# A one-core mixer-and-FFN layer: modulation rows turned by a transpose before they are stored, first convolution taps moved from VectorE to ScalarE, two blocks of modulation sums moved to TensorE, and one gate's sums moved later

## The chip, the core and the metric

The kernel runs on one core of a Trainium2 chip. The metric is the device time of one execution in microseconds (us). Before the change the median of three runs is 2446.79 us (2441.33 to 2446.85). The names of the engines in the profile are PE (TensorE matmul), PEld (TensorE's weight load, which runs beside matmuls), DVE (VectorE), ACT (ScalarE), POOL (GpSimd) and SP (SyncE, whose queue issues nearly all DMAs here).

## What is computed

One layer acts on x of 2048 tokens by 1024 features, steered by one vector c of 1024. Silu of c times a 1024 x 6144 matrix gives six modulation rows; a second matrix gives two more for the closing norm.

```
c_act = silu(c)
shift_m, scale_m, gate_m, shift_f, scale_f, gate_f = split(c_act @ w_ada + b_ada, 6)
h = rms_norm(x, g_mix) * (1 + scale_m) + shift_m
gate_b, gate_c, h_conv, q, k, v, z, a, bt = split(h @ w_in)
ya = grouped_rms(gate_b * conv3(gate_c * h_conv))
q, k, v = split(silu(conv4([q, k, v])))           # causal, depthwise
o = chunked_gated_delta_rule(l2(q), l2(k), v, g(a), sigmoid(bt))
yb = rms_norm(o) * silu(z)
x = x + gate_m * ([ya, yb] @ w_out)
h = rms_norm(x, g_ffn) * (1 + scale_f) + shift_f
x = x + gate_f * ((silu(h @ w_gate) * (h @ w_up)) @ w_down)
out = rms_norm(x, g_final) * (1 + scale_o) + shift_o
```

All tensors are float32. A product is made of three passes over a high and a low part of each operand (high by high, high by low, low by high), so each weight tile is first cast on ScalarE (`whi`, L367) and its rest taken on VectorE (`wlo`, L369).

## The kernel before

**Stages.** The mixer works on four blocks of 512 tokens (`for b in range(NB)`, about 0 to 1114 us of the profile), then come the gate-and-up products of the feed-forward part (to about 1982 us) and the down products. In a block the projections come strip by strip, a strip being the 128 output features of one 1024 x 128 piece of `w_in`: four of k, four of q, four of v, four of z, then twelve for the gated convolution, then the output product. A strip is 24 matmuls of 128 x 128 by 128 x 512 (`proj`). Beside them, small generators ("chains", `head_chain`, `q_chain`, `chunk_chain` and so on) build the delta rule's inverse and walk its four chunks of 128 tokens; `tick()` lets one of them go on between matmuls.

**Order.** A planner (`Clock`) gives each instruction a cost and notes when it would begin. From the first k strip to the end of the mixer (`clock.pinned`) the order on every engine and queue is fixed to the planner's order; in the front (before that) and in the feed-forward stage the compiler's list scheduler chooses it. Every engine, and SP's queue, then works in order: an instruction that waits holds up all behind it.

**Weights and background work.** `fill(n)` requests strips ahead: each request loads a strip into one of four `wraw` buffers (L362), splits it, and lets one step of the background deque `bg` run. A background generator `mod_gen(v, fin)` makes modulation row v: it loads c_act broadcast to 128 partitions (L443), then eight pieces of 512 KB of `w_ada` (L447), and for each runs one VectorE multiply-and-sum (`sums_of`, L438) into one column of a 128 x 8 tile `ms`. Both use the same four `wraw` buffers in the mixer (three `y` buffers in the feed-forward stage). Then `fin` runs. For rows that are needed along the free axis it is `to_row` (L458 to L460): add the bias, and store the 128 x 8 tile to a 4 KB row in DRAM, feature p + 128k from element (p, k), so that every element of 4 bytes is a piece of its own. Four rows go this way: `gate_md` (from L786's `mod_gen(2, ...)`, queued in front of block 0; it is read back broadcast into `gate_m`, L785, and first used at 281.3 us, when block 0's output product is scaled, L1312), `gate_fd` (in block 2), and `go_d` and `so_d` (in the feed-forward stage, one step for each of its second half's 22 strips, `bg_step`).

**The front.** SP's queue loads the four x tiles of block 0, then pieces k = 0, 1, 2 of shift and scale weights (1 MB each, `ada_load`, L705) with three strips between them, then piece 3. ScalarE computes Silu of c (broadcast, 512 KB, `crow`), norms the x tiles (`x_norm`, L470 and L701); for each k, VectorE takes two sums of 1024 (`ada_sums`), ScalarE makes the scale and shift columns `Gm`, `Sm` of feature block k, TensorE turns the x tiles (L493), `scale_split` makes `hTh`, `hTl`, and the first five k and q strips (`pre`) run their matmuls of that k.

**Convolutions.** `conv` (L1156 to L1163) reads a projection from PSUM: the first instruction, tap n, is a VectorE multiply by a per-partition scalar (L1159), the other taps are three (for q, k, v) or two multiply-adds on VectorE (L1161), then three columns of halo are added (L1163). There are 16 a block, 64 in all. Their PSUM bank is one of four.

Of the kernel before, what the change touches and what calls it, by code (L numbers as in the profile page):

```python
# [38 lines left out]
KPS = 0, 2, 3, 1  # L39
POLL = -1  # L40
HALF = 1024
COLS = (("b_sm", 8), ("b_cm", 8), ("g_mix", 8), ("g_ffn", 8), ("b_sf", 8), ("b_cf", 8), ("b_gm", 8), ("b_gf", 8), ("b_so", 8),
        ("b_go", 8), ("cw_mix", 12), ("cw_qkv", 48), ("g_conv", 4), ("g_dn", 1))
NCOLS = sum(n for _, n in COLS)
# [166 lines left out]


@with_exitstack
def layer_kernel(ctx, tc, x, c, w_ada, cols, g_norm_final, w_in, w_ab, a_log, dt_bias, w_out, w_gate_up,
                 w_down, cst, out):
    nc = tc.nc
    x, out = x[0], out[0]
# [219 lines left out]
    def sums_of(raw, row, total):  # L437
        nc.vector.scalar_tensor_tensor(raw, raw, 1.0, row, op0=ALU.mult, op1=ALU.mult, accum_out=total)  # L438

    def mod_gen(v, fin):  # L440
        row = temp()
        clock.kept.add(row.name)
        nc.sync.dma_start(row, c_d.to_broadcast([P, D]))  # L443
        sums = g0.tile([P, KD], F32, name="ms", bufs=2)
        for k in range(KD):
            raw = temp()
            nc.sync.dma_start(raw, w_ada[v, k])  # L447
            sums_of(raw, row, sums[:, k:k + 1])
            yield
        clock.kept.discard(row.name)  # L450
        fin(sums)

    def to_col(sums, bias, t, gain=None):
        nc.vector.tensor_add(t, sums, bias)
# [2 lines left out]

    def to_row(sums, bias, t):  # L458
        nc.vector.tensor_add(sums, sums, bias)
        nc.sync.dma_start(t.rearrange("o (k p) -> p (o k)", p=P), sums)  # L460


    def rms_scale(ss, n, n_el):
# [191 lines left out]
    with ExitStack() as actx:  # L655
# [45 lines left out]
                    nc.scalar.activation(xt0[i - 1], xt0[i - 1], AF.Identity, scale=ss[i - 1])  # L701

        def ada_load(k):
            t = ap_.tile([P, 2, D], F32, name=PLACES[k % 4])
            nc.sync.dma_start(t, w_ada[0:2, k].rearrange("s p n -> p s n"))  # L705
            return t

        def ada_sums(k, raw):
            sums_of(raw[:, 1], crow, totals[1][:, k:k + 1])
            sums_of(raw[:, 0], crow, totals[0][:, k:k + 1])  # L710
            nc.scalar.activation(Gm[:, k:k + 1], totals[1][:, k:k + 1], AF.Identity,
                                 scale=col["g_mix"][:, k:k + 1], bias=gb[:, k:k + 1])
            nc.scalar.activation(Sm[:, k:k + 1], totals[0][:, k:k + 1], AF.Identity, bias=col["b_sm"][:, k:k + 1])

        def proj_ab(ps, ks):
            for k in ks:
# [9 lines left out]
            return hl[:, 0], hl[:, 1]  # L726

        nc.scalar.dma_start(crow, c.to_broadcast([P, D]))
        nc.scalar.activation(totals[0], epsc.to_broadcast([P, KD]), AF.Silu)
        nc.scalar.activation(crow, crow, AF.Silu)  # L730
        nc.scalar.dma_start(c_d, crow[0:1, :])
        for i in range(CH):
            x_load(i)
        raws, strips = [], []
        for k in range(3):
            raws.append(ada_load(k))
            strips.append(next(reqs)[0](w_in, 2048 + k * P))
        raws.append(ada_load(3))
        x_norm()
        wab = g0.tile([P, KD, 8], F32, name="wab")  # L740
        nc.sync.dma_start(wab, w_ab)
# [39 lines left out]
        gate_md = dr.tile([1, D], F32, name="gate_md")  # L781

        def gate_row(sums):
            to_row(sums, col["b_gm"], gate_md)
            nc.sync.dma_start(gate_m, gate_md.to_broadcast([P, D]))  # L785
        bg.append(mod_gen(2, gate_row))  # L786

        for b in range(NB):
            hh, hl = hT
# [366 lines left out]

            def conv(cv, u, taps, back):
                n = len(taps) - 1
                nc.vector.tensor_scalar_mul(cv, u, taps[n])  # L1159
                for t in range(n - 1, -1, -1):  # L1160
                    nc.vector.scalar_tensor_tensor(cv[:, n - t:], u[:, :BLK - n + t], taps[t], cv[:, n - t:],  # L1161
                                                   op0=ALU.mult, op1=ALU.add)
                nc.vector.tensor_add(cv[:, :n], cv[:, :n], back)  # L1163
# [19 lines left out]
            for key, c0, dstT in (("k", 2048, kT), ("q", 1536, qT), ("v", 2560, None)):  # L1183
                clock.pinned = clock.pinned or key == "k"
                for h in range(NH):
                    m = (c0 - 1536) // P + h
                    if pre:
                        w, ps = pre.pop(0)
                        proj(ps, w, hh, hl, LAST)
                        clock.kept.discard(ps.name)  # L1190
                        fill(min(NH - len(pre), PRE + 1))
                    else:
                        w, ps = next_w(), dense_ps()
                        proj(ps, w, hh, hl)
                    take_now("cv", 1)
                    cv = cv_tile([P, BLK])
                    conv(cv, ps, [col["cw_qkv"][:, t * 12 + m:t * 12 + m + 1] for t in range(4)], halo[:, m, :])
                    nc.vector.tensor_copy(edge[:, m, :], ps[:, BLK - 3:])
                    nc.scalar.activation(cv if dstT is None else dstT[:, h, :], cv, AF.Silu)
                    done[key] += 1  # L1200
                    if dstT is not None:
                        give("cv", 1)
                    else:
                        spawn(v_chain(h, cv), 1)
            spawn(chunk_chain(), 1)
            halo_terms(nhalo, edge, col["cw_qkv"])

# [653 lines left out]
def laid_out(v):  # L1861
    f = {n: np.asarray(a) for n, a in v.items()}
    given = {n: f[n] for n in ("x", "c")}
    ada = np.concatenate([f["w_ada"][0], f["w_ada_final"]], axis=1)
    given["w_ada"] = ada.T.reshape(8, KD, P, D)
    b_ada, b_fin = f["b_ada"].reshape(-1, P), f["b_ada_final"].reshape(-1, P)
# [29 lines left out]
```

## Time and profile before

| | |
|---|---|
| median of three runs | 2446.79 us |
| the profiled execution | 2436.84 us |
| its span, first to last instruction | 2435.0 us |
| mean granted TensorE clock | 0.988 |
| busy: PE, DVE, ACT, POOL | 2333.2, 1782.0, 1041.9, 568.5 us |
| HBM read and written | 269.92 and 75.52 MB |

Busy time is the union of an engine's instruction records; PE's records overlap, since matmuls are pipelined. The view of waits names for each waiting instruction the one that released it, with "total, times, longest". A row of the timeline gives start, duration, engine, line, operation, output<-inputs, and in brackets the idle time before it and its releaser. A row of windows gives a stretch's length, then each engine's busy time and instruction count, the granted clock, the DMA share and the rate in GB/s. A row of groups gives count, busy time, mean ns of one, idle time before and its releasers.

### The profile page before, as it was taken

How to read it: one execution, taken by the hardware profiler on the slowest of the kernel's cores; microseconds unless marked ns; L12 is line 12 of the kernel's file. 1: busy time of each engine (PE TensorE's matmuls, PEld its weight loads, DVE VectorE, ACT ScalarE, POOL GpSimd, SP SyncE). 2: the span in 40 equal slices, each digit the busy share in tenths (PEclk: the TensorE clock that was granted, in tenths of full speed). 3: DMA queues.
4: the chain of work that ended last, by engine and by line, in shares of the span. 5: the costliest groups of instructions: out<-in, count | busy, mean ns of one | idle time of the engine just before them, and what ended most of it. 6: DMA issues, size and time to landing. Idle time of an engine off the chain costs nothing.

```text
span 2435.0 us, 30701 instructions
## 1 busy us (share of the span) xinstructions
PE 2333.2 (96%) x11192; PEld 1925.8 (79%) x11192; DVE 1782.0 (73%) x2697; ACT 1041.9 (43%) x1784; POOL 568.5 (23%) x642
## 2 busy tenths in 40 slices
PE   6999899989999999999999999989999999999997
PEld 4787787877878888887878888868888877887786
DVE  5978689875877678787666566866556569878887
ACT  6444564444634564356543333523333323322345
POOL 0340444022521262111000000000000036434447
PEclk9999999999999999999999999989999999999999
DMA  7443455524662535245663334774433365333433
GB/s 275 125 131 97 145 185 174 173 87 130 163 152 71 165 124 156 63 153 159 200 211 110 99 108 115 250 156 119 111 93 111 98 224 175 114 121 120 134 126 150
DMA packets 216412, 345.37 MB, mean 142 GB/s; under 512 B 42498, under 2 KB 134914, under 8 KB 216195
## 3 DMA queue, kind: packets, MB, share of 16 engines
q1 hardware_dynamic: 214528, 340.37, 46.0%
q0 software_dynamic: 1152, 2.10, 0.6%
q8 instruction: 88, 1.44, 0.2%
q10 hardware_dynamic: 578, 0.93, 0.1%
q14 instruction: 66, 0.53, 0.1%
HBM read 269.92 MB, written 75.52 MB: 142 GB/s over the span
## 4 chain that ended last, share of the span: by engine, by line
PE 65%; DVE 16%; DMA 8%; ACT 5%; issue 4%; POOL 3%; SPq 0%; DVEq 0%; POOLq 0%; ACTq 0%
PE pd L324 41%; PE pm L324 17%; DVE wlo L369 3%; DVE cv L1161 2%; DMA y<-in_w_ada_dram 1%; DVE acc L1733 1%; DMA y<-xT 1%; DVE wraw L438 1%; ACT whi L367 1%; DMA wraw<-in_w_in_dram 1%; DVE cv L1159 1%; DVE cv L1234 1%; DMA A12d<-y 1%; PE pm L1003 1%; PE pm L995 1%
## 5 line engine op out<-in xcount | busy, mean ns | idle before, releaser
L367 ACT CAST whi<-wraw 128x1024 fp32r<-128x1024 f32 x285 | 298.5, 1049 | 418.9 <-PE pd L324 187.2
L369 DVE TENSOR_TENSOR wlo<-wraw,whi 128x1024 fp32r<-128x1024 f32 x285 | 361.0, 1268 | 102.7 <-ACT whi L367 100.4
L324 PE MATMUL pd<-hTh,whi 128*128 128x512 f32 x888 | 360.6, 407 | 1.4 <-ACT hTh L498 1.3
L324 PE MATMUL pd<-hTh,wlo 128*128 128x512 f32 x888 | 349.5, 394 | 5.9 <-DVE wlo L369 5.9
L324 PE MATMUL pd<-hTl,whi 128*128 128x512 f32 x888 | 348.6, 393 | 0.0
L324 PEld LDWEIGHTS pd<-hTh,wlo 128*128 128x128 f32 x888 | 168.0, 189 | 44.0 <-DVE wlo L369 7.9
L324 PEld LDWEIGHTS pd<-hTh,whi 128*128 128x128 f32 x888 | 168.6, 190 | 34.2 <-ACT hTh L498 1.9
L324 PEld LDWEIGHTS pd<-hTl,whi 128*128 128x128 f32 x888 | 168.6, 190 | 31.0 <-DVE hTl L499 0.4
L1475 DVE TENSOR_TENSOR sg<-sg,pd 128x512 f32<-128x512 f32 x44 | 30.2, 687 | 172.3 <-PE pd L324 171.7
L1733 DVE TENSOR_TENSOR acc<-acc,pd 128x512 f32<-128x512 f32 x192 | 127.4, 679 | 25.6 <-PE pd L324 24.3
L1613 ACT CAST xh<-ra 128x640 fp32r<-128x640 f32 (+1 forms) x85 | 60.4, 722 | 184.4 <-PE pm L324 138.9
L1161 DVE SCALAR_TENSOR_TENSOR cv<-pd,pc,cv 128x511 f32<-128x511 f32 (+2 forms) x173 | 129.3, 748 | 5.2
L1535 POOL TENSOR_TENSOR ht<-y,ht 128x512 fp32r<-128x512 f32 x1 | 1.3, 1290 | 461.4 <-DMA y<-act 461.4
L324 PE MATMUL pd<-whi,ym 128*128 128x512 f32 x256 | 89.2, 409 | 9.7 <-ACT ym L1150 9.7
L1622 POOL TENSOR_TENSOR xl<-ra,xh 128x640 fp32r<-128x640 f32 (+1 forms) x37 | 62.1, 1679 | 144.4 <-ACT xh L1613 134.9
L1733 DVE TENSOR_TENSOR acc<-acc,pm 128x512 f32<-128x512 f32 x120 | 81.6, 680 | 18.2 <-PE pm L324 17.9
L324 PE MATMUL pd<-A22h,whi 128*128 128x512 f32 x176 | 70.2, 399 | 13.8 <-DVE sg L1475 13.8
L1527 POOL TENSOR_TENSOR wraw<-wraw 128x1024 f32<-128x1024 f32 x2 | 5.4, 2678 | 324.7 <-DMA wraw<-in_w_down_dram 324.7
L1662 POOL TENSOR_TENSOR wraw<-wraw 128x512 f32<-128x512 f32 x40 | 68.0, 1726 | 51.7 <-DMA wraw<-in_w_down_dram 30.7
L324 PE MATMUL pm<-S1h,whi 128*128 128x512 f32 x176 | 69.4, 394 | 1.2 <-ACT whi L367 1.2
L324 PE MATMUL pd<-S2h,whi 128*128 128x512 f32 x176 | 69.3, 394 | 1.0 <-ACT whi L367 1.0
L324 PE MATMUL pd<-S2h,wlo 128*128 128x512 f32 x176 | 69.3, 394 | 0.5 <-DVE wlo L369 0.5
(430 smaller groups left out, 6239.7 us busy)
## 6 DMA issues: line engine op xcount, KB each, us to landing
wraw<-in_w_in_dram SPq DMA_DIRECT2D x112, 512.0 KB, 4.2
wraw<-in_w_gate_up_dram SPq DMA_DIRECT2D x88, 512.0 KB, 3.8
ra<-act SPq DMA_DIRECT2D x80, 448.0 KB, 3.7
wraw<-in_w_out_dram SPq DMA_DIRECT2D x40, 512.0 KB, 3.6
act<-S SPq DMA_DIRECT2D x80, 256.0 KB, 2.8
act<-act SPq DMA_DIRECT2D x68, 256.0 KB, 2.2
wraw<-in_w_ada_dram SPq DMA_DIRECT2D x32, 512.0 KB, 4.4
wraw<-in_w_down_dram SPq DMA_DIRECT2D x22, 512.0 KB, 3.9
```

Of the source, the lines that this page charges most:

```text
L324: mm(*args, **kw)
L367: nc.scalar.copy(hi, raw)
L369: (lo_engines.popleft() if lo_engines else nc.vector).tensor_sub(lo, raw, hi.bitcast(F32))
L438: nc.vector.scalar_tensor_tensor(raw, raw, 1.0, row, op0=ALU.mult, op1=ALU.mult, accum_out=total)
L995: mm(py[:, j * P:(j + 1) * P], Mm[h][:, j, :], T[h][:, j, :], start=True, stop=True)
L1003: mm(pz[:, j * P:(j + 1) * P], Y[h][:, j, :], Xs[h][:, j, :], start=True, stop=True)
L1161: nc.vector.scalar_tensor_tensor(cv[:, n - t:], u[:, :BLK - n + t], taps[t], cv[:, n - t:], op0=ALU.mult, op1=ALU.add)
L1475: nc.vector.tensor_add(s5[i], s5[i], a[i])
L1613: nc.scalar.copy(hi, raw[:, c0:c1, :])
L1622: eng.tensor_sub(lo, raw, hi.bitcast(F32))
L1662: nc.gpsimd.tensor_mul(r[:, hs], r[:, hs], gate_f[:, hs])
L1733: nc.vector.tensor_add(accs[s, u][:, ns], accs[s, u][:, ns], ps)
```

## The change

Five edits are made together.

1. `to_row` adds the bias, lets at least two more background steps pass (`settled`; in the pinned part also until the planner's time is 2 us past the sums), turns the 128 x 8 sums by one TensorE transpose into 8 x 128 in PSUM, copies that to SBUF on ScalarE, and stores it as eight pieces of 512 bytes.
2. The first tap of every convolution is an `activation(Identity, scale=tap)` on ScalarE, from PSUM to SBUF.
3. In the front, feature blocks k = 0 and 1 come in another layout (`w_first`, `c_col`, made on the host: 128 inputs on partitions), and their sums are 16 matmuls each of 128 x 128 by 128 x 1 into PSUM columns, with Silu of `c_col` as the moving operand. The loads are reordered: piece 0, x tiles 0 and 1, piece 1, x tiles 2 and 3, strip 0, piece 2, strip 1, piece 3, strip 2.
4. `mod_gen(2, gate_row)` is queued after block 0's v strips in place of ahead of the block.
5. While the five prepared strips are used up, one strip more is requested: `NH + 1 - len(pre)`.

```diff
     def mod_gen(v, fin):
...
-        fin(sums)
+        yield from fin(sums) or ()
+
+    def settled(*tiles):
+        yield
+        yield
+        while clock.pinned and due(tiles, 0) + 2 > clock.pe:
+            yield
...
     def to_row(sums, bias, t):
         nc.vector.tensor_add(sums, sums, bias)
-        nc.sync.dma_start(t.rearrange("o (k p) -> p (o k)", p=P), sums)
+        yield from settled(sums)
+        ps = misc_ps()
+        nc.tensor.transpose(ps[:KD, :P], sums, ident)
+        row = sp.tile([P, BLK], F32, name="ht", bufs=2)[:KD, :P]
+        nc.scalar.copy(row, ps[:KD, :P])
+        nc.sync.dma_start(t.rearrange("o (k p) -> (o k) p", p=P), row)
...
         def ada_load(k):
-            t = ap_.tile([P, 2, D], F32, name=PLACES[k % 4])
-            nc.sync.dma_start(t, w_ada[0:2, k].rearrange("s p n -> p s n"))
+            if k < AHEAD:
+                t = ap_.tile([P, 2, KD, P], F32, name=PLACES[k % 4])
+                nc.sync.dma_start(t, w_first[k])
+            else:
+                t = ap_.tile([P, 2, D], F32, name=PLACES[k % 4])
+                nc.sync.dma_start(t, w_ada[0:2, k].rearrange("s p n -> p s n"))
             return t

         def ada_sums(k, raw):
-            sums_of(raw[:, 1], crow, totals[1][:, k:k + 1])
-            sums_of(raw[:, 0], crow, totals[0][:, k:k + 1])
...
+            if k < AHEAD:
+                ps = misc_ps()
+                sums = [ps[:, s:s + 1] for s in range(2)]
+                for s in (1, 0):
+                    for i in range(KD):
+                        mm(sums[s], raw[:, s, i, :], cs[:, i:i + 1], start=s == 1 and i == 0, stop=i == KD - 1,
+                           skip_group_check=True)
+            else:
+                sums = [t[:, k:k + 1] for t in totals]
+                for s in (1, 0):
+                    sums_of(raw[:, s], crow, sums[s])
...
         nc.scalar.dma_start(crow, c.to_broadcast([P, D]))
-        nc.scalar.activation(totals[0], epsc.to_broadcast([P, KD]), AF.Silu)
+        cs = Gf
+        nc.scalar.dma_start(cs, c_col)
+        nc.scalar.activation(cs, cs, AF.Silu)
...
-        for i in range(CH):
-            x_load(i)
-        raws, strips = [], []
-        for k in range(3):
-            raws.append(ada_load(k))
-            strips.append(next(reqs)[0](w_in, 2048 + k * P))
+        raws, strips = [ada_load(0)], []
+        x_load(0)
+        x_load(1)
+        raws.append(ada_load(1))
+        x_load(2)
+        x_load(3)
+        strips.append(next(reqs)[0](w_in, 2048))
+        raws.append(ada_load(2))
+        strips.append(next(reqs)[0](w_in, 2048 + P))
         raws.append(ada_load(3))
+        strips.append(next(reqs)[0](w_in, 2048 + 2 * P))
...
         def gate_row(sums):
-            to_row(sums, col["b_gm"], gate_md)
+            yield from to_row(sums, col["b_gm"], gate_md)
             nc.sync.dma_start(gate_m, gate_md.to_broadcast([P, D]))
-        bg.append(mod_gen(2, gate_row))
...
             def conv(cv, u, taps, back):
                 n = len(taps) - 1
-                nc.vector.tensor_scalar_mul(cv, u, taps[n])
+                nc.scalar.activation(cv, u, AF.Identity, scale=taps[n])
...
-                        fill(min(NH - len(pre), PRE + 1))
+                        fill(min(NH + 1 - len(pre), PRE + 1))
...
+            if b == 0:
+                bg.append(mod_gen(2, gate_row))
             spawn(chunk_chain(), 1)
```

More of the change, by code (lines that the diff above doesn't have):

```diff
@@ L41 @@
 HALF = 1024
+AHEAD = 2
 COLS = (("b_sm", 8), ("b_cm", 8), ("g_mix", 8), ("g_ffn", 8), ("b_sf", 8), ("b_cf", 8), ("b_gm", 8), ("b_gf", 8), ("b_so", 8),
@@ L213, in layer_kernel @@
 @with_exitstack
-def layer_kernel(ctx, tc, x, c, w_ada, cols, g_norm_final, w_in, w_ab, a_log, dt_bias, w_out, w_gate_up,
+def layer_kernel(ctx, tc, x, c, w_ada, c_col, w_first, cols, g_norm_final, w_in, w_ab, a_log, dt_bias, w_out, w_gate_up,
                  w_down, cst, out):
@@ L703, in ada_load @@
         def ada_load(k):
-            t = ap_.tile([P, 2, D], F32, name=PLACES[k % 4])
-            nc.sync.dma_start(t, w_ada[0:2, k].rearrange("s p n -> p s n"))
+            if k < AHEAD:
[4 more added lines that the diff above has]
+                nc.sync.dma_start(t, w_ada[0:2, k].rearrange("s p n -> p s n"))
             return t
         def ada_sums(k, raw):
-            sums_of(raw[:, 1], crow, totals[1][:, k:k + 1])
-            sums_of(raw[:, 0], crow, totals[0][:, k:k + 1])
-            nc.scalar.activation(Gm[:, k:k + 1], totals[1][:, k:k + 1], AF.Identity,
-                                 scale=col["g_mix"][:, k:k + 1], bias=gb[:, k:k + 1])
-            nc.scalar.activation(Sm[:, k:k + 1], totals[0][:, k:k + 1], AF.Identity, bias=col["b_sm"][:, k:k + 1])
+            if k < AHEAD:
[9 more added lines that the diff above has]
+                    sums_of(raw[:, s], crow, sums[s])
+            nc.scalar.activation(Gm[:, k:k + 1], sums[1], AF.Identity, scale=col["g_mix"][:, k:k + 1], bias=gb[:, k:k + 1])
+            nc.scalar.activation(Sm[:, k:k + 1], sums[0], AF.Identity, bias=col["b_sm"][:, k:k + 1])
         def proj_ab(ps, ks):
@@ L1865, in laid_out @@
     given["w_ada"] = ada.T.reshape(8, KD, P, D)
+    given["c_col"] = f["c"].reshape(KD, P).T
+    given["w_first"] = ada[:, :2 * D].reshape(KD, P, 2, KD, P)[:, :, :, :AHEAD].transpose(3, 1, 2, 0, 4)
     b_ada, b_fin = f["b_ada"].reshape(-1, P), f["b_ada_final"].reshape(-1, P)
```

## The prediction, made before the changed kernel was built or run

> **What bounds the kernel now.** I read the busy times first, then who TensorE waits for, then the stretches around its longest waits.
>
> ```profile
> span 2435.0 us, 30701 instructions
> ## 1 busy us (share of the span) xinstructions
> PE 2333.2 (96%) x11192; PEld 1925.8 (79%) x11192; DVE 1782.0 (73%) x2697; ACT 1041.9 (43%) x1784; POOL 568.5 (23%) x642
> ```
>
> TensorE is busy in all but 2435.0 - 2333.2 = 101.8 us, and the change takes none of its matmuls away. So nearly all that can be won lies in these 101.8 us and in the half clock that follows a long wait. TensorE's waits, longest totals first (total, times, longest):
>
> ```profile
> PE pm L493 <- ACT kq L701: 17.0, 3, 14.1
> PE pd L324 <- DVE sg L1475: 13.8, 4, 10.2
> PE pd L324 <- DVE acc L1733: 10.8, 9, 2.0
> PE pd L324 <- ACT ym L1150: 9.7, 4, 3.4
> PE pm L828 <- ACT cv L1199: 8.6, 4, 2.9
> PE pm L1144 <- POOL ch L1139: 7.4, 3, 5.9
> PE pd L324 <- DVE wlo L369: 7.2, 5, 4.9
> PE pm L1231 <- DVE lv L1226: 3.2, 2, 2.9
> PE pm L828 <- DVE kd L917: 2.8, 1, 2.8
> ```
>
> The 17.0 is the front, until x is normed. The single wait of 10.2 lies in the feed-forward stage. L369, L828 and L1231 are waits inside blocks for a late VectorE or for ScalarE behind it. L1150 and L1144 are the ends of blocks 0 and 1, where TensorE has run out of other work and follows the delta-rule chain. L1733 is the down stage, which the change doesn't touch. The stretches (length, then busy time of PE, PEld, DVE, ACT, POOL, then granted clock, DMA share, GB/s):
>
> ```profile
> 0.00:22.37 22.37, 4.38 (x16) 2.85 (x16) 6.60 (x15) 14.07 (x22) 3.82 (x15) 1.00 0.93 362
> 60.00:80.00 20.00, 15.13 (x55) 11.96 (x55) 19.06 (x39) 5.01 (x7) 7.78 (x9) 0.83 0.36 107
> 130.00:190.00 60.00, 57.25 (x283) 48.04 (x281) 48.23 (x111) 22.47 (x62) 21.99 (x26) 0.98 0.36 105
> 238.00:264.00 26.00, 18.04 (x132) 15.41 (x129) 14.47 (x23) 5.45 (x20) 7.78 (x14) 0.93 0.07 21
> 534.00:554.00 20.00, 9.27 (x41) 7.07 (x40) 7.53 (x11) 10.74 (x22) 6.59 (x14) 0.78 0.13 40
> ```
>
> At 60 to 80 us VectorE is the bound (19.06 of 20). The two block ends (238 and 534) lose 26.00 - 18.04 = 8.0 and 20.00 - 9.27 = 10.7 us, with every engine half idle: a chain of latencies.
>
> **1. Rows stored in 8 pieces in place of 1024.** The wait of 10.2 us comes from the store of `go_d`. SP's queue, VectorE, the chain of waits, and the landing of L460's store and of an ordinary load:
>
> ```profile
> 1593.86 0.36 SPq L460 DMA_DIRECT2D go_d<-ms  x1
> 1594.27 1.96 SPq L447 DMA_DIRECT2D y<-in_w_ada_dram  x2
> ```
> ```profile
> 1607.25 1.23 DVE L438 SCALAR_TENSOR_TENSOR y<-y 128x1024 f32<-128x1024 f32 x1 [8.47 <-DMA y<-in_w_ada_dram]
> ```
> ```profile
> 1614.89 8.31 PE pd L324 x24
> 1636.80 5.44 PE pd L324 x24
> ```
> ```profile
> DMA to landing us min/median/max: 12.2/12.2/12.2
> ```
> ```profile
> y<-in_w_ada_dram SPq DMA_DIRECT2D x16, 512.0 KB, 5.0
> ```
> ```profile
> out_dram<-acc SPq DMA_DIRECT2D x3, 256.0 KB, 2.0
> ```
>
> The store of 4 KB takes 12.2 us, and the load issued 0.41 us behind it lands at 1607.25, 13.0 us after its issue, where 5.0 is usual. VectorE stands in front of its sum for 8.47 us with TensorE's next accumulation (L1475) queued behind. TensorE waits 10.2 and then takes 8.31 for 24 matmuls that otherwise take 5.44: 2.9 more, 13.1 in all. Without the slow store the load lands at 1599.3. Two more loads and sums still stand ahead of L1475, the last of them issued only when a buffer comes free; by the 5.0 and the 1.2 of a sum they end near 1607 and not at 1614, which leaves 2 to 3 us of the wait. The 2.9 goes, if so short a wait leaves the clock up. **Taken: -10** (bounds 0, if the bunched loads alone hold VectorE, to -13). The row of 8 pieces has no like here; the nearest is a 256 KB store with 2.0 us, so I take about 2 us against 12.2, hidden: nobody reads `go_d` for hundreds of us. What is added is a transpose, one ScalarE copy and a wait on TensorE's queue for the sums; the two background steps between put it behind them.
>
> In block 0 `gate_md` is read back at once, and SP stands still for it; ScalarE's cast behind it, and with it the squares of the k heads, stand too. In block 2 `gate_fd` holds up the strip behind it (an ordinary one lands in 4.2):
>
> ```profile
> SPq L785 <- DMA gate_md<-ms: 10.3, 1, 10.3
> ```
> ```profile
> 125.33 1.04 ACT L367 CAST whi<-wraw 128x1024 fp32r<-128x1024 f32 x1 [6.60 <-DMA wraw<-in_w_in_dram]
> ```
> ```profile
> 678.17 1.04 ACT L367 CAST whi<-wraw 128x1024 fp32r<-128x1024 f32 x1 [6.21 <-DMA wraw<-in_w_in_dram]
> ```
> ```profile
> wraw<-in_w_in_dram SPq DMA_DIRECT2D x112, 512.0 KB, 4.2
> ```
>
> Block 0's share is the wait on L917, 2.8 us. In block 2, two of L828's four waits on L1199 (8.6 in all, the longest 2.9) follow the late cast; I give them half. **Taken: -2.8 and -4** (bounds 0 to -2.8; 0 to -6).
>
> **2. First taps on ScalarE.** VectorE, then ScalarE's nearest forms, and its casts:
>
> ```profile
> L1159 DVE TENSOR_SCALAR cv<-pd,pc 128x512 f32<-128x512 f32 x63 | 46.8, 744 | 10.4 <-PE pd L324 10.3
> ```
> ```profile
> L497 ACT ACTIVATE pm<-pm,Sm,Gm 128x512 f32<-128x512 f32 x32 | 24.1, 754 | 6.0 <-PE pm L493 5.9
> ```
> ```profile
> L1248 ACT COPY cv<-pd 128x512 f32<-128x512 f32 x16 | 9.4, 585 | 29.7 <-PE pd L324 29.7
> ```
> ```profile
> L367 ACT CAST whi<-wraw 128x1024 fp32r<-128x1024 f32 x285 | 298.5, 1049 | 418.9 <-PE pd L324 187.2 <-PE pm L324 151.6 <-DMA wraw<-in_w_in_dram 44.7
> ```
>
> 64 x 0.744 = 47.6 us leave VectorE and 64 x 0.585 to 0.754 = 37 to 48 us come to ScalarE, which is 43% busy. One per-partition operand lies between the two forms: I take 0.66, 42 us. A handoff is added to each convolution, which the next VectorE work covers. The twelve q, k, v taps of a block are 8.9 us off VectorE where it is the bound. In blocks 1 and 2 this goes against the other half of L828's wait on L1199 (4.3) and the end of block 1 (10.7), whose chain starts earlier. **Taken: -3 and -3** (bounds: +6, if the handoffs show, to -12).
>
> The Trainium skill, "ScalarE: Activation LUTs", section "Rules for kernel authors", speaks against this: it sends multiplications to VectorE. By its figures (section "What ACT_TABLE_LOAD costs": 186 ns, 0.833 ns an element, 93 ns for a pointer operand) the estimate is 186 + 427 + 93 = 706 ns; by the rule the edit would gain nothing, while the rows, 585 to 754 against 744, make the two engines equal, and what counts is which one is free.
>
> **3. Front and start of block 0.** Here VectorE loses the sums of the gate row (8 x 1.41), the taps, and the split of strip 5 is requested ahead of the first convolution:
>
> ```profile
> L438 DVE SCALAR_TENSOR_TENSOR wraw<-wraw 128x1024 f32<-128x1024 f32 x32 | 45.1, 1409 | 1.1 <-DMA wraw<-in_w_ada_dram 1.1
> ```
> ```profile
> 63.40 1.92 DVE L369 TENSOR_TENSOR wlo<-wraw,whi 128x1024 fp32r<-128x1024 f32 x1
> ```
>
> TensorE waits 4.9 us for this `wlo`, which ends at 65.3 us. With one sum (1.4) and one tap (0.7) gone from ahead of it the wait is 2.8; put ahead of the convolution too, it is gone. A wait under 3 us spares the slow matmuls after it (2.9, as in the feed-forward row). **Taken: -6** (bounds -2 to -7.8).
>
> For the front, whose first product starts at 22.37 us (the end of the first stretch above): ScalarE's chain, and the nearest row to the new sums:
>
> ```profile
> 16.01 1.04 ACT L470 ACTIVATE ht<-kq 128x1024 bf16<-128x1024 f32 x1
> 16.96 0.18 ACT L470 ACTIVATION_READ_ACCUMULATOR ht<-kq 128x1 f32 x1
> 17.05 1.03 ACT L367 CAST whi<-wraw 128x1024 fp32r<-128x1024 f32 x1
> 17.98 2.18 ACT L701 ACTIVATE kq<-kq,ss 128x1024 f32<-128x1024 f32 x2
> ```
> ```profile
> 87.98 0.29 PE L888 MATMUL pm<-g,ck 128*128 128x16 f32 x2
> ```
>
> Ahead of the last x tile now lie 2 MB more: pieces 0 and 1. With x, Silu's row and the small loads 4.8 MB at 362 GB/s are 13.3 us, and with some 2 us of start it lands at about 15.3. Its square, power and scaling take at most 1.97 + 1.09 = 3.1, so x is normed at 18.4 where it is 20.16 now. The new sums are 32 matmuls of at most 0.29 (two passes each, as in the last row): 9.3 us at full clock, 18.6 at half. Piece 0's half of them, 4.6 to 9.3, falls before 18.4, while TensorE has only turns to do (4.38 busy of 22.37); piece 1's may run on beside the first products, which is the upper bound. VectorE's 4 sums less shorten what follows. **Taken: -1.5** (bounds +5 to -4).
>
> The same skill, "TensorE: Matmul & The Clock Gate", Part 1, says that an idle window of about 3.4 us halves TensorE's clock and a busy one restores it; by it the early sums would leave the first products warm, up to the 2.9 us more that the feed-forward row shows for a cold start. I leave that out of the sum.
>
> **4. Gate sums later.** 8 x 1.41 = 11.3 us of VectorE and nine loads come into 130 to 190 us, where VectorE has 48.23 of 60 and loses 4 x 0.74 by taps. They fit (57 of 60), but the delta-rule chain's 62 small VectorE steps and its four DMA round trips on SP's queue lie there as well. `gate_m` is in time: 11 steps of 5.4 us from about 130, against its use at 281.3. I charge **+4**: the end of block 0 (8.0 lost now) is reached earlier by TensorE, by items 1 to 3, and the chain gains less. For the planner's new order, of either sign, **+1**.
>
> **Sum:** -10 - 2.8 - 4 - 3 - 3 - 6 - 1.5 + 4 + 1 = -25.3. The profiled execution took 2436.84 (1.84 outside its span) and would take 2411.5; the median of the runs is 10 us higher, 2446.79, and the forecast for it is 2446.8 - 25.3 = **2421.5**.
>
> **The rivals.**
> - *The block ends decide.* TensorE's gains in blocks 0 and 1 are given back where it waits for the chain. For it: 8.0 and 10.7 us are lost there with all engines half idle. Against: the chain of block 0 itself stands behind the 6.60 us cast and the bound VectorE. It leaves items outside those ends: -10 - 4, +1: 2433.8.
> - *The chains gain more than TensorE.* Both ends shrink by half, 9 us, and the +4 goes: 2446.8 - 25.3 - 4 - 9 = 2408.5.
> - *The slow store isn't the cause*, the bunched loads are; then -10 becomes -2 and block 2's -4 becomes -1: 2432.5. Against: only the two loads behind it took 13.
> - *Slower: taps behind casts.* ScalarE works in order, and a tap queued behind a cast waits for that cast's strip. Casts wait 44.7 us for `w_in` strips; passed on through VectorE, 91 to 95% busy in these phases, to TensorE they would cost up to 44.7: 2446.8 - 25.3 + 44.7 = 2466. It makes the kernel slower by 0.3% once over 25.3 + 7.3 = 33 us of it pass on. Against: 13 of the 44.7 are the two rows' stores, and a cast waits because strips come early, not late.
>
> **How the numbers follow.** A difference of 0.3% is 7.3 us, about what a measurement of this kernel can tell from none: below 2439.5 is faster, above 2454.1 slower. Chances: forecast 0.52, block ends 0.20, chains gain more 0.09, store not the cause 0.09, taps behind casts 0.10. The last case reaches from same to slower, half and half; of the block ends and the store a fifth ends within 0.3%, and so does 0.01 of the forecast: same 0.05 + 0.06 + 0.01 = 0.12, slower 0.05, faster 0.83. The range reaches from the chains' case with the larger bounds, 2403, to the block ends with some new waits, 2442.
>
> **What would show it.** Right: no wait of TensorE over 4 us between 1590 and 1640 us; ScalarE 38 to 48 us busier, VectorE 50 to 60 less (47.6 and four sums); no 12 us landing on L460's successor; `wlo` of strip 5 ready before 61 us; no cast waiting 6 us near 125 and 678. Wrong: TensorE's idle time grows at the ends of blocks 0 and 1 (L1144, L1150) by what the blocks won; a new wait of TensorE on the sums before a transpose; VectorE waiting on ScalarE before L1161 for over 20 us in total.

## The result and the profile after

| | before | after |
|---|---|---|
| median | 2446.36 us (2441.33 to 2446.85, 4 runs) | 2411.27 us (2409.5 to 2411.49, 4 runs) |
| ratio of the medians, 95% interval | | 0.986 [0.9842, 0.9877] |
| profiled execution | 2436.84 us | 2411.49 us |
| TensorE idle in the span | 101.8 us | 72.3 us |

Faster: by 35 us between the medians, by 25.35 between the two profiled executions. The two differ because the profiled execution of before was shorter than all four of its timed runs. The busy line of the page after:

```profile
span 2409.7 us, 30846 instructions
...
PE 2337.4 (97%) x11260; PEld 1933.7 (80%) x11260; DVE 1732.6 (72%) x2625; ACT 1082.6 (45%) x1854; POOL 568.3 (24%) x642
```

ScalarE is 40.7 us busier and VectorE 49.4 less, as the moved taps and sums should make it. TensorE idles 2409.7 - 2337.4 = 72.3 us, 29.5 less than before, and is busy 4.2 us more. Who it waits for (total, times, longest):

```profile
PE pm L505 <- ACT kq L713: 18.5, 3, 16.2
PE pd L325 <- DVE acc L1764: 11.0, 11, 2.0
PE pd L325 <- DVE sg L1506: 5.9, 4, 3.0
PE pm L857 <- ACT cv L1228: 4.3, 3, 3.5
PE pd L325 <- DVE edge L1227: 3.0, 1, 3.0
...
PE pd L325 <- ACT ym L1179: 2.0, 1, 2.0
...
PE pm L1173 <- POOL ch L1168: 1.5, 3, 0.9
```

Lines have moved: L505 was L493, L1506 was L1475, L857 was L828, L1179 was L1150, L1173 was L1144. The feed-forward wait of 10.2 is down to 3.0, the wait on the late `wlo` has left the list's head (a wait of 3.0 on L1227 stands in its place), and the two waits at the ends of blocks 0 and 1 have gone from 9.7 and 7.4 to 2.0 and 1.5. The front's wait is no shorter. Three of the stretches shown for before, the front again up to its first product:

```profile
0.00:37.78 37.78, 17.79 (x81) 16.19 (x81) 4.23 (x11) 14.90 (x24) 3.83 (x15) 1.00 0.83 305
...
238.00:264.00 26.00, 26.00 (x168) 23.26 (x167) 21.12 (x29) 12.44 (x31) 13.21 (x25) 1.00 0.37 121
534.00:554.00 20.00, 16.46 (x76) 12.86 (x75) 12.16 (x13) 15.26 (x24) 3.91 (x7) 0.83 0.18 54
```

The first row is the surprise: the first product starts at 37.78 us, 15.4 later than before. From there all of that and 25 us more is won back. Block 0's end (238 to 264) has no hole left, block 1's (534 to 554) 3.5 us in place of 10.7. What happened in the front, by TensorE's timeline:

```profile
16.18 0.47 PE L505 MATMUL pm<-ck,kq 128*128 128x128 f32 x1 [16.18 <-ACT kq L713]
16.45 6.83 PE L730 MATMUL pm<-Gf,kd 128*128 128x1 f32 x32
23.13 0.45 PE L505 MATMUL pm<-ck,kq 128*128 128x128 f32 x1
23.38 5.12 PE L730 MATMUL pm<-Gf,vt 128*128 128x1 f32 x24
...
28.82 1.71 PE L730 MATMUL pm<-Gf,vt 128*128 128x1 f32 x8
...
35.28 1.11 PE L505 MATMUL pm<-ck,kq 128*128 128x128 f32 x4 [2.01 <-ACT kq L713]
37.78 0.80 PE L325 MATMUL pd<-hTh,whi 128*128 128x512 f32 x1 [1.38 <-ACT hTh L510]
```

L730 are the new sums. The first turn stands ahead of them, so they begin at 16.45, although their moving operand was ready at 13.0 (Silu of `c_col`, L755); each of the two feature blocks then takes 6.83 us. ScalarE's timeline:

```profile
14.98 2.19 ACT L713 ACTIVATE kq<-kq,ss 128x1024 f32<-128x1024 f32 x2
23.31 0.35 ACT L736 ACTIVATE Gm<-pm,gb,pc 128x1 f32<-128x1 f32 x1 [6.14 <-PE pm L730]
...
23.70 1.05 ACT L482 ACTIVATE ht<-kq 128x1024 bf16<-128x1024 f32 x1
...
30.56 0.35 ACT L736 ACTIVATE Gm<-pm,gb,pc 128x1 f32<-128x1 f32 x1 [5.72 <-PE pm L730]
...
32.00 1.05 ACT L482 ACTIVATE ht<-kq 128x1024 bf16<-128x1024 f32 x1
```

ScalarE works in order too. It waits 6.14 and 5.72 us for the sums to make `Gm`, and the squares of x tiles 2 and 3 (L482 at 23.70 and 32.00) stand behind those waits, though both tiles had landed by 15.1. So the last x tile is turned at 35.28 us, when before is long in its products. And VectorE, from which the sums were taken:

```profile
34.10 1.23 DVE L370 TENSOR_TENSOR wlo<-wraw,whi 128x1024 fp32r<-128x1024 f32 x1 [26.44 <-ACT whi L368]
```

It stands idle for 26.44 us.

### The profile page after: what moved, and what is told of

It reads as the page before. It is cut to its first block, busy times and chain, and to the rows that moved or that the text cites. A ratio compares the mean times of both kernels' runs of the same rounds, so it can differ in the third digit from the quotient of the medians.

```text
span 2409.7 us, 30846 instructions
## 1 busy us (share of the span) xinstructions
PE 2337.4 (97%) x11260; PEld 1933.7 (80%) x11260; DVE 1732.6 (72%) x2625; ACT 1082.6 (45%) x1854; POOL 568.3 (24%) x642
## 5 line engine op out<-in xcount | busy, mean ns | idle before, releaser
L1506 DVE TENSOR_TENSOR sg<-sg,pd 128x512 f32<-128x512 f32 x44 | 30.2, 687 | 172.1 <-PE pd L325 171.5
L1764 DVE TENSOR_TENSOR acc<-acc,pd 128x512 f32<-128x512 f32 x192 | 127.4, 679 | 25.6 <-PE pd L325 25.2
L1764 DVE TENSOR_TENSOR acc<-acc,pm 128x512 f32<-128x512 f32 x120 | 81.7, 681 | 18.4 <-PE pm L325 18.1
L325 PE MATMUL pm<-S1h,wlo 128*128 128x512 f32 x176 | 69.3, 394 | 0.5 <-DVE wlo L370 0.5
L325 PE MATMUL pd<-A22l,whi 128*128 128x512 f32 x176 | 69.2, 393 | 0.0
```

The costliest lines, as they stand in the source:

```text
L325: mm(*args, **kw)
L1506: nc.vector.tensor_add(s5[i], s5[i], a[i])
L1764: nc.vector.tensor_add(accs[s, u][:, ns], accs[s, u][:, ns], ps)
```

## The experiments

**Theory.** The front costs some 15 us, by the sums' place in two in-order queues and by their length; the taps are worth far more than forecast, because VectorE's work in blocks 0 and 1 sets when the delta-rule chain ends; the rows are worth about what was forecast. **Rivals.** The late front is hidden behind VectorE-bound block 0, and so costs nothing at the end; the place of the gate's sums, not the taps, emptied the block ends; the pieces' place in the queue, not their size, is what the rows gain.

Each ratio below is to before, run on the same chip. The table shows where each kernel's profiled execution stands, in us: the first product, the start of the last output scaling of each block, the 24th and 25th feed-forward sums of L1475 (between them lies the wait of 10.2), the first down sum, and the span.

| kernel | first product | block 0 | block 1 | block 2 | block 3 | sum 24 | sum 25 | down | span |
|---|---|---|---|---|---|---|---|---|---|
| before | 22.4 | 315.3 | 592.2 | 858.3 | 1114.7 | 1584.7 | 1614.2 | 1987.6 | 2435.0 |
| after | 37.8 | 309.5 | 581.3 | 843.0 | 1099.4 | 1568.3 | 1590.6 | 1963.4 | 2409.7 |
| old front (e1) | 22.4 | 293.9 | 564.1 | 826.3 | 1082.3 | 1554.2 | 1576.3 | 1949.1 | 2395.7 |
| 4-byte rows (e2) | 37.9 | 317.0 | 588.3 | 855.0 | 1110.6 | 1580.6 | 1610.2 | 1983.0 | 2430.2 |
| taps on VectorE (e3) | 37.8 | 324.1 | 606.4 | 868.8 | 1125.1 | 1593.6 | 1615.5 | 1986.6 | 2432.3 |
| early gate sums (e4) | 38.1 | 312.0 | 585.6 | 848.3 | 1103.8 | 1573.6 | 1595.1 | 1966.4 | 2410.9 |
| late 4-byte rows (e5) | 37.9 | 308.4 | 581.2 | 851.9 | 1107.7 | 1577.5 | 1599.3 | 1974.8 | 2420.8 |
| front alone (e6) | 37.8 | 331.2 | 613.9 | 881.5 | 1137.8 | 1609.0 | 1639.5 | 2013.2 | 2461.2 |
| taps alone (e7) | 22.5 | 300.3 | 567.8 | 835.2 | 1090.9 | 1564.9 | 1593.5 | 1966.2 | 2412.9 |

**The front: undone, and alone.** After without its new front (the loads' order, `w_first`, `c_col`, the sums on TensorE), and before with nothing else but that front:

```diff
-            if k < AHEAD:
...
-                        mm(sums[s], raw[:, s, i, :], cs[:, i:i + 1], start=s == 1 and i == 0, stop=i == KD - 1,
-                           skip_group_check=True)
...
+            sums_of(raw[:, 1], crow, totals[1][:, k:k + 1])
+            sums_of(raw[:, 0], crow, totals[0][:, k:k + 1])
...
-        raws, strips = [ada_load(0)], []
-        x_load(0)
...
+        for i in range(CH):
+            x_load(i)
```

> All of the change but its front: the x tiles are loaded first and all eight feature blocks are summed on VectorE again. In the changed kernel the first product starts at 37.8 us, 15.4 later than before. Theory: the sums on TensorE, with ScalarE's norms queued behind them, cost those 15 us, and block 0, whose end no longer waits for the delta-rule chain, passes them on; without them the first product is back near 22 us and the median falls by 10 to 16 us, to 2395 to 2401. Rival: block 0 is set by its chain, so an earlier front only lengthens a wait at the end of block 0 (as before, 8.0 us in 238 to 264); then 2406 to 2411.

> The kernel before with the new front alone (load order, two blocks' sums on TensorE). Theory: the first product comes 15 us later, at 37.8, but the end of block 0, which waits for the delta-rule chain there, takes up part: 5 to 15 us slower than before on the same chip, ratio 1.002 to 1.006. Rival: the 4 sums less on VectorE let the front end no later; ratio 0.998 to 1.001.

Without it: 2391.88 us (2387.8 to 2397.43), ratio 0.9804 [0.9767, 0.9841]. That is 19.4 below after by the medians, which come from different sets of runs, and 14 by the ratios and by the spans. Alone: 2457.82 us, ratio 1.0073 [1.0048, 1.0097], 19.5 above before, more than the 5 to 15 that were expected. The table shows the 15.4 us of delay reaching the end of block 0 whole (309.5 - 293.9 = 15.6; 331.2 - 315.3 = 15.9) and staying: 14.0 are left in the one span, and 26.2 have come of it in the other. Nothing hides it.

**What in the front costs it.** Three kernels take after's front apart: the `Gm` and `Sm` columns of the two TensorE blocks made on VectorE, so that ScalarE doesn't wait; the old order of the loads with the sums left on TensorE; and the new order of the loads with all sums on VectorE.

```diff
             if k < AHEAD:
+                nc.vector.scalar_tensor_tensor(Gm[:, k:k + 1], sums[1], col["g_mix"][:, k:k + 1], gb[:, k:k + 1],
+                                               op0=ALU.mult, op1=ALU.add)
+                nc.vector.tensor_add(Sm[:, k:k + 1], sums[0], col["b_sm"][:, k:k + 1])
```

> The changed kernel with the scale and shift columns of the two TensorE blocks made on VectorE, which is idle there, in place of ScalarE. In the changed kernel ScalarE stands 6.1 and 5.7 us for TensorE's sums at the first block's and the second block's column, with the squares and scalings of x tiles 2 and 3 behind it. Theory: with that wait off ScalarE, x is normed by about 24 us, and the first product is set by TensorE's 64 sums, which end at 30.2: it starts at 31 to 33 and the median falls by 4 to 7 us, to 2404 to 2407. Rival: TensorE's sums set it anyway (they keep half clock and stand ahead of the turns), 0 to 2 us: 2409 to 2412.

> The changed kernel with the loads in the order of before (x first), the two blocks' sums still on TensorE. Theory: the 64 matmul passes at 0.21 us each, 13.9 us, stand in TensorE's queue ahead of the first product wherever x comes, so it starts at 28 to 34 us and the median is 2401 to 2408. Rival: the load order is the cause, x comes too late; then the first product is at 22 to 25 us and the median 2391 to 2398.

> The changed kernel with its new load order, but all eight blocks' sums on VectorE. Theory (TensorE's sums are the cause): the first product starts at 21 to 26 us and the median is 2390 to 2398. Rival (the load order is the cause): it starts at 30 us or later, 2400 to 2409.

| kernel | first product | span | median | ratio |
|---|---|---|---|---|
| after | 37.8 | 2409.7 | 2411.27 | 0.986 [0.9842, 0.9877] |
| columns on VectorE (e8) | 34.8 | 2403.5 | 2406.21 | 0.986 [0.9833, 0.9886] |
| old loads, TensorE sums (e10) | 32.8 | 2403.5 | 2405.44 | 0.9849 [0.9831, 0.9867] |
| new loads, VectorE sums (e11) | 27.4 | 2394.8 | 2398.83 | 0.9816 [0.979, 0.9841] |
| old loads, VectorE sums (e1) | 22.4 | 2395.7 | 2391.88 | 0.9804 [0.9767, 0.9841] |

So of the 15.4 us by which the first product is late the sums on TensorE are 10.4 (37.8 - 27.4, and 32.8 - 22.4 under the old loads), and the order of the loads 5.0 (37.8 - 32.8, and 27.4 - 22.4). The two add up. In the whole time the sums are worth 11 us by the ratios and 12 to 14 by the medians; the loads' 3 by the ratios and 6 to 7 by the medians aren't clear of the intervals. Of the sums' share 3.0 is ScalarE's wait; that this shortens the whole is not shown, since e8's ratio is after's. The rest shows in TensorE's timeline of e10, where x was normed early and the turns still stand behind the sums:

```profile
15.48 6.83 PE L730 MATMUL pm<-Gf,kd 128*128 128x1 f32 x32
22.17 1.31 PE L505 MATMUL pm<-ck,kq 128*128 128x128 f32 x5
23.27 6.83 PE L730 MATMUL pm<-Gf,vt 128*128 128x1 f32 x32
29.95 1.52 PE L505 MATMUL pm<-ck,kq 128*128 128x128 f32 x6
```

For e8 the first product was expected at 31 to 33 and came at 34.8: x is normed at 23.5 there, but the turns of its last tiles still stand behind the sums. For e11 it was expected at 21 to 26 and came at 27.4, far nearer to that than to the rival's 30 or later.

**The taps: undone, alone, and in two blocks only.**

```diff
                 n = len(taps) - 1
-                nc.scalar.activation(cv, u, AF.Identity, scale=taps[n])
+                nc.vector.tensor_scalar_mul(cv, u, taps[n])
```

> The changed kernel with the first tap of all 64 convolutions on VectorE again. Theory: VectorE is the bound in the k, q, v phases and 8.9 us a block go back onto it, so blocks 0 to 2 lose 2 to 5 us each: 2417 to 2426. Rival: the taps are worth nothing, since the two engines take the same time and VectorE's wait for ScalarE (27 us before L1190 in the changed kernel) eats the 47 us saved: 2408 to 2414.

> The kernel before with the first taps on ScalarE alone. Theory: VectorE and the delta-rule chain on it set blocks 0 and 1, so the taps alone bring most of what undoing them cost, 18 to 26 us: ratio 0.989 to 0.993. Rival: they only matter together with the gate sums' move and the early strip; alone 0 to 8 us, ratio 0.997 to 1.000.

Undone: 2435.45 us (10 runs), ratio 0.9973 [0.9954, 0.9991], so 24.2 above after, more than any side had expected. Alone, in before: 2413.16 us (2411.34 to 2414.69), ratio 0.9888 [0.9868, 0.9907], 25.2 below before. The table puts it into blocks 0 and 1: undone, 14.6 and then 25.1 us are lost by their ends, and no more after that; alone, 15.0 and then 24.4 are won. The page and two of TensorE's waits with the taps on VectorE:

```profile
span 2432.3 us, 30846 instructions
...
PE 2344.5 (96%) x11260; PEld 1938.7 (80%) x11260; DVE 1769.2 (73%) x2689; ACT 1045.0 (43%) x1790; POOL 568.7 (23%) x642
```
```profile
PE pd L325 <- ACT ym L1179: 9.1, 4, 3.4
PE pm L1173 <- POOL ch L1168: 7.2, 2, 5.9
```

TensorE is idle 2432.3 - 2344.5 = 87.8 us, 15.5 more than after, and 9.1 + 7.2 - 2.0 - 1.5 = 12.8 of that are the waits on the chain at the ends of blocks 0 and 1. The other 7.1 us of the 22.6 are busy time: the same number of matmuls, taking longer. With the taps alone in before both waits are nearly gone:

```profile
PE pd L324 <- ACT ym L1150: 2.0, 1, 2.0
...
PE pm L1144 <- POOL ch L1139: 1.9, 4, 0.9
```

The delta-rule chain itself runs earlier. These are its products (`Mm` by `T`) in block 0, before and with the taps alone:

```profile
L995 PE MATMUL pm<-lv,ym x32: 272/275/275, 217.7 to 221.1; 128*128 128x128 f32 x32
```
```profile
L995 PE MATMUL pm<-lv,ym x32: 272/275/276, 194.7 to 198.2; 128*128 128x128 f32 x32
```

They come 23.0 us earlier, and the last cast of `ym` in block 1 (L1150) starts at 525.2 and not at 551.9. With the taps undone in after, the same products begin 18.3 us later (224.1, 205.8).

The third kernel keeps the taps on ScalarE in blocks 0 and 1 alone:

```diff
-                nc.scalar.activation(cv, u, AF.Identity, scale=taps[n])
+                if b < 2:
+                    nc.scalar.activation(cv, u, AF.Identity, scale=taps[n])
+                else:
+                    nc.vector.tensor_scalar_mul(cv, u, taps[n])
```

> The changed kernel with first taps on ScalarE in blocks 0 and 1 alone, on VectorE in blocks 2 and 3. Theory: the taps pay where TensorE waits at the block's end for the delta-rule chain, whose small steps queue on VectorE, and that was in blocks 0 and 1 alone; so nothing is lost: 2408 to 2415. Rival: they pay wherever VectorE is over 90% busy, in each block's k, q, v phase; then half of the 24 us is lost: 2420 to 2426.

2411.33 us (2408.51 to 2412.26), ratio 0.9869 [0.9848, 0.989]: after's time, with block ends at 843.3 and 1099.8 where after has 843.0 and 1099.4. The other 32 taps are worth nothing that these runs can tell, on either engine. What pays is VectorE time in the two blocks where TensorE runs out of other work and follows the chain.

**The rows: 4-byte pieces again, and 4-byte pieces in the new place.** In the first the 128 x 8 tile is stored as before; the second keeps the transpose, the copy and the later place, and changes only the pieces, and with them the order in which the row's elements lie in DRAM.

```diff
-        ps = misc_ps()
-        nc.tensor.transpose(ps[:KD, :P], sums, ident)
...
-        nc.sync.dma_start(t.rearrange("o (k p) -> (o k) p", p=P), row)
+        nc.sync.dma_start(t.rearrange("o (k p) -> p (o k)", p=P), sums)
```
```diff
-        nc.sync.dma_start(t.rearrange("o (k p) -> (o k) p", p=P), row)
+        nc.sync.dma_start(t.rearrange("o (p k) -> (o k) p", k=KD), row)
```

> The changed kernel with the four rows stored straight from the 128 x 8 sums again, in 1024 pieces, at the changed kernel's places in the program; transpose and copy are gone. Theory: the slow store delays the loads behind it by about 8 us each time, VectorE stands for them in the feed-forward stage and TensorE waits 7 to 10 us there, with 3 to 8 more in blocks 0 and 2: 2421 to 2431. Rival: the bunched loads of the last two rows are the cause and the store adds little: 2411 to 2415.

> The changed kernel, transpose, copy and late places kept, but the 8 x 128 row is stored in 1024 pieces of 4 bytes (the DRAM side is permuted, so the rows' elements come in another order). In the changed kernel go_d's store is issued at 1731 us, where no loads are bunched, and not at 1594. Theory A, the pieces cost where loads queue behind them: no wait returns in the feed-forward stage, since nothing is bunched behind the late store; blocks 0 and 2 lose 3 to 8 us together: 2414 to 2420. Theory B, the place does not matter, the pieces alone do: TensorE waits about 7 us in the feed-forward stage again: 2421 to 2430. Rival C, neither: 2409 to 2413.

The first takes 2430.32 us (10 runs), ratio 0.9949 [0.9931, 0.9967], 19.1 above after; the second 2419.01 us, ratio 0.9913 [0.9891, 0.9934], 7.7 above. The first loses in three places (table): 7.5 us by the end of block 0, 4.5 more by the end of block 2, 7.3 between sums 24 and 25. Its waits have the old 10.2 back:

```profile
PE pd L325 <- DVE sg L1502: 13.6, 4, 10.2
...
PE pm L1257 <- ACT lv L1252: 6.8, 2, 5.7
PE pm L1068 <- ACT junkd L859: 4.1, 1, 4.1
```

The two waits below it are of the delta-rule chains: the 5.7 lies at 210 us in block 0, the 4.1 at 671 us in block 2. SP's queue shows the cause of the first, the chain's second round trip standing behind the gate's (e2, then after with its block 2 too):

```profile
183.40 0.38 SPq L468 DMA_DIRECT2D gate_md<-ms  x1
...
197.97 0.33 SPq L811 DMA_DIRECT2D gate_m<-gate_md  x1
198.40 2.93 SPq L989 DMA_DIRECT2D Dg<-dx  x2
```
```profile
191.16 1.47 SPq L993 DMA_DIRECT2D Dg<-dx  x2
194.29 0.35 SPq L472 DMA_DIRECT2D gate_md<-ht  x1
196.81 0.36 SPq L815 DMA_DIRECT2D gate_m<-gate_md  x1
...
660.18 0.32 SPq L472 DMA_DIRECT2D gate_fd<-ht  x1
661.38 0.39 SPq L969 DMA_DIRECT2D dm<-Dg  x1
665.12 1.11 SPq L974 DMA_DIRECT2D yal<-dm  x2
```

From the row's store to its read-back e2 takes 14.6 us and after 2.5; `Dg`'s load waits in the queue meanwhile. The second kernel, in block 2:

```profile
661.43 0.33 SPq L472 DMA_DIRECT2D gate_fd<-ht  x1
662.64 2.03 SPq L969 DMA_DIRECT2D dm<-Dg  x1
673.65 1.11 SPq L974 DMA_DIRECT2D yal<-dm  x2
```

Here the chain's store of `dm`, issued 1.2 us behind the row, is read back 11.0 us later and not 3.7: the size of the pieces by itself, and block 2 ends 8.9 us later than after's (table). Block 0 loses nothing by them (308.4, 309.5). Nor does the feed-forward stage at sum 25. There TensorE is full, the transposes come late in its queue, and `go_d` leaves at 1739.5 us (after: 1730.8) where before stored it at 1593.86, among a bunch of loads. So in that stage the place alone removes the wait; in block 2 the pieces do.

**The gate's sums early again.**

```diff
             nc.sync.dma_start(gate_m, gate_md.to_broadcast([P, D]))
+        bg.append(mod_gen(2, gate_row))
...
-            if b == 0:
-                bg.append(mod_gen(2, gate_row))
```

> The changed kernel with the gate row's sums queued ahead of block 0 again. Theory: 11 us of VectorE come back into the start of block 0, where it is the bound, and its delta-rule chain starts later: 2415 to 2423. Rival: their place does not matter, VectorE's total in the block is the same: 2409 to 2413.

2411.6 us (2406.38 to 2414.05), ratio 0.988 [0.9844, 0.9917]: after's time within the interval. In its profile the mixer ends 4.4 us later than after's and the span 1.2, so the later place costs nothing that the runs can tell; whether it gains a little is open.

**The old request of strips**, in e1:

```diff
-                        fill(min(NH + 1 - len(pre), PRE + 1))
+                        fill(min(NH - len(pre), PRE + 1))
```

> e1 (all of the change but its front) with the strips requested as before while the five prepared ones are used up. Theory: the one earlier split is what takes TensorE's 4.9 us wait for strip 5 away at the start of block 0, so that wait comes back in part, 2 to 5 us, and block 0 passes it on: 2394 to 2398. Rival: with the gate sums and the taps gone from VectorE the split is in time anyway: 2389 to 2393.

2394.03 us (2392.83 to 2399.42), ratio 0.9806 [0.9786, 0.9826], against e1's 0.9804. Block 0 ends at 292.7 and 293.9. The edit makes no difference to the time that these runs can tell, although it does what it was made for at strip 5. TensorE with the old request (e9), then with the new one (e1):

```profile
62.49 0.50 PE L324 MATMUL pd<-hTh,whi 128*128 128x512 f32 x1 [2.71 <-ACT whi L367]
...
65.45 0.79 PE L324 MATMUL pd<-hTh,wlo 128*128 128x512 f32 x1 [2.23 <-DVE wlo L369]
```
```profile
61.03 0.47 PE L324 MATMUL pd<-hTh,whi 128*128 128x512 f32 x1 [1.32 <-DVE sp_s L875]
```

The two waits of e9, 4.9 us together, are the size of before's single one; in e1 they are gone.

e1, after with the old front, beats both kernels; e11 lies within its interval.

## Why the prediction was right, and where it was not

The forecast of 2421.5 stands 10.2 us above the median, inside its range; against the profiled execution it is -25.3 where -25.35 came. That second agreement is an accident: two terms failed, by about 17 and 16 us, against each other. What the edits are worth when each is undone in after, by the spans (14.0 lost by the front; 22.6 won by the taps, 20.5 by the rows, 1.2 by the gate sums' place), sums to 5 us more gain than came. The effects may overlap, or the single executions spread by that much; the runs don't say.

- **The front, -1.5 with bounds +5 to -4: failed, it is +15.4.** The step that failed is "piece 0's half of them, 4.6 to 9.3, falls before 18.4, while TensorE has only turns to do". The sums' price was near enough, 13.66 us for the 32 matmuls between 9.3 and 18.6. Their place was not. The first turn stood ahead of them until 16.18, the other turns behind them, and ScalarE waited for them with x tiles 2 and 3 still to norm, so 10.4 us of the two halves lay on the path. The free engine there was VectorE. A second step failed with it. The last x tile landed at 15.1, as the text said (15.3), but the 3.1 us for its square, power and scaling left out that two tiles arrive and stand in line: in e8, where ScalarE doesn't wait for the sums, x is normed at 23.5 and not at 18.4. So the order of the loads, priced at a gain of 1.8, costs 5.0.
- **First taps, -3 and -3 with bounds to -12: the right mechanism, mis-sized; they are -22.6** (undone) to -22.1 (alone) by the spans. The forecast said block 1's "chain starts earlier", and priced TensorE's named waits. It left out that block 0's end is the same case, that the gain of an earlier chain comes once in each of the two blocks, and that 7.1 us are matmuls that run slower without the edit. That the taps pay in these two blocks alone is shown (e12), and that the chain comes earlier by them, by 18 to 23 us in block 0; which of its VectorE steps wait for the taps was not taken apart. VectorE does wait for ScalarE's taps, by more than the 20 us that were to prove the forecast wrong (multiply-adds, then taps):

```profile
L1190 DVE SCALAR_TENSOR_TENSOR cv<-pd,pc,cv 128x511 f32<-128x511 f32 x63 | 46.8, 744 | 27.4 <-ACT cv L1188 27.2
...
L1188 ACT ACTIVATE cv<-pd,pc 128x512 f32<-128x512 f32 x63 | 43.0, 685 | 44.5 <-PE pd L325 30.8 <-DVE uedge L1285 13.3
```

  The taps gained all the same: that sign was badly chosen. A tap takes 0.685, against 0.66 taken. The Trainium skill's "ScalarE: Activation LUTs", in "What ACT_TABLE_LOAD costs", gives the 706 ns estimated, which the trace bears out to about 3%; its rule to keep multiplications on VectorE ("Rules for kernel authors") the runs contradict here.
- **Rows, -10, -2.8 and -4: right in sum, 16.8 against the 20.5 of the spans** in e2. The feed-forward wait fell to 3.0 where 2 to 3 us were to be left. Its condition, that "so short a wait leaves the clock up", did not hold: the granted clock is 0.50 in the stretch 1591.5 to 1594.8 behind that wait. Block 0's share in e2 is 7.5 and not 2.8, but for another place: there the row is stored at 183 us and holds up the chain's own transfers on SP's queue, while the step priced the old place, 110.9 us, by L917's wait. No run undoes the rows at the old place. That the store leaves its bunch was not foreseen, and is enough by itself in the feed-forward stage (e5).
- **Start of block 0, -6: the wait went as forecast, but its worth at the block's end is not shown.** The 4.9 us wait for strip 5's `wlo` is gone in e1, and the request ahead of the convolution is needed for it (e9). But e9's block 0 ends no later. VectorE does gain: with the same front, e1 begins the fifth convolution's halo at 79.6 us where before has 86.3. The taps alone account for 3.3 of these 6.7 us (83.0), the request of strip 5 for none (79.6 without it). Of the rest, the gate's sums, gone from ahead of block 0, are the likeliest source: with them early (e4) the same point comes 3.9 us later than after's (99.3, 95.4). The rule behind the term, "A wait under 3 us spares the slow matmuls after it", fails in before itself: TensorE's waits of 2.8 us at 128 and 2.9 at 190 us are followed by a granted clock of 0.50 (128.8 to 132.2, and 190.3 to 193.6).
- **Gate sums later, +4: failed, it costs nothing** (e4). The failed words are "the chain gains less": with the taps gone from VectorE the chain hardly sets the blocks' ends, as the two waits there show (2.0 and 1.5).
- **Planner's order, +1:** too small to be seen.

Of the rivals, "the chains gain more than TensorE" (2408.5) describes what happened to blocks 0 and 1, more strongly than it was priced, and its time is nearer to the 2411.27 than the forecast's. "The block ends decide" fell with the waits at L1173 and L1179. "Taps behind casts" did not come: the taps made the kernel faster. "The slow store isn't the cause" is half true in the feed-forward stage, and false elsewhere.

## What to carry to other kernels

Before work moves to another engine, ask what the giving engine does in that stretch and what stands behind the work in the taking engine's queue: sums taken from an idle VectorE and put ahead of TensorE's first turns put the first product off by 10 us, although they are short and TensorE was mostly idle. Where TensorE ends a stage by following a chain, work taken off an engine that the chain uses can be worth more than the waits that TensorE's list names: here 22 us against 17. A store of many tiny pieces can be paid by whoever issues a transfer behind it on that queue, so look at what stands there.

## What the runs showed of the hardware that was not expected

The products with one moving column came at the pace of a slow TensorE, and did not speed it up. The loads of the new sums' weights, and those of the nearest row that the forecast used (L888, before):

```profile
L730 PEld LDWEIGHTS pm<-Gf,kd x32: 333/333/391, 16.2 to 22.9; 128*128 128x128 f32 x32
```
```profile
L888 PEld LDWEIGHTS pm<-g,ck x8: 187/190/193, 87.7 to 871.2; 128*128 128x128 f32 x8
```

They take 333 ns against 190 and overlap; a pass comes every 6.83/32 = 0.213 us. Fourteen us of such passes left TensorE slow: in after the products behind them come 0.43 us apart until 45.13 us, and 0.23 apart from there, while the view's granted clock reads 1.00 (the trace's first record of the clock begins at 45.2 us; the view counts what is ahead of it as full). The Trainium skill's "TensorE: Matmul & The Clock Gate", Part 1, has a busy window of about 3.4 us restore the clock; by it the products should have started fast. The trace disagrees for this kind of work. In e8 twelve turns in a row stand behind the sums:

```profile
30.47 2.91 PE L505 MATMUL pm<-ck,kq 128*128 128x128 f32 x12
```

There the clock's first record, at full, begins at 33.4 us, and the products at 36.53 and 36.77 are 0.24 us apart. Some 3 us of turns did what 14 us of such passes had not, in this one trace; after the short waits among those products the granted clock is 0.51 from 36.8 to 40.3.

The load of 4 KB for `c_col`, issued at 2.13 us, landed about 12.7, when Silu could start, with 4 MB and more requested beside it. Before's executions spread from 2430.84 to 2451.33 us over 19 runs, where after's four agree within 2 us; why was not tried.
